# mLSTM heads: low parts of filler weights from an accumulating transfer instead of a VectorE subtraction

## The chip, the cores and the metric

The kernel runs on one core of a Trainium2 chip. The metric is the device time of one execution in microseconds (us); lower is better. TensorE multiplies, VectorE and ScalarE do element-wise work, GpSimd does small work and issues some transfers, SyncE issues most transfers. In the profile they are PE (with PEld for its weight loads), DVE, ACT, POOL and SP.

## What is computed

One decoder layer over 512 tokens of width 1024, float32 throughout:

```python
hN = _rmsnorm(x, norm_g[l])
p = _split_in(hN @ w_in[l])
mq = silu(_causal_dwconv(p["m_q"], conv_q_w[l], conv_q_b[l]))
mk = silu(_causal_dwconv(p["m_k"], conv_k_w[l], conv_k_b[l]))
mh = _mlstm(mq, mk, p["m_v"], p["m_i"] + b_igate[l], p["m_f"] + b_fgate[l])   # 4 heads x 256
ya = sigmoid(p["m_o"]) * _head_layernorm(mh, mh_norm_g[l]) * silu(p["m_z"])
...
yb = _nsa(...) * silu(p["n_z"])                                               # 8 heads x 64
merged = sigmoid(p["g_a"]) * (ya @ w_branch_a[l]) + sigmoid(p["g_b"]) * (yb @ w_branch_b[l])
x = x + merged @ w_out[l]
return _rmsnorm(x, final_norm_g)
```

The part that matters here is the mLSTM branch: for each of four heads the projections to queries and keys, a causal convolution of width 4 with SiLU, scores weighted by the gates' decay, and the products with the values.

## The kernel before

**Products in three passes.** TensorE multiplies in a rounded 32-bit format. To keep the precision of float32, each operand is split into a high part, rounded to that format, and a low part, the difference. A product is three: high x high, high x low, low x high. `split(src, hi, lo)` makes the parts: ScalarE copies `src` into `hi` (which rounds it), then VectorE subtracts, `lo = src - hi`.

**Weights.** `weights(src)` loads a 512 KB tile of weights with SyncE into a raw tile (`wr`, three buffers), and calls `split` for the high part (`wh`, four buffers) and the low part (`wl`, four buffers). A raw buffer is free for the next load when both parts are made; a pair `wh`, `wl` is free when TensorE is done with it. In SyncE's queue a load waits for the release of its raw buffer.

**Filler.** The kernel is arranged so that TensorE always has work. Projections that are not urgent stand in a list of jobs, `stream`. A job is a weight tile and 24 products of 512 columns (12 for branch B); `stream.step(n)` emits n products of it between products of the main work, and at the end of a job its `post` step. When a job is started, the weights of the two jobs behind it are fetched (`Stream(2)`).

**The mLSTM stage.** The list of jobs is: for each head h four `conv` jobs (queries and keys, each in two halves e), 16 in all, then eight `branch` jobs for branch B, which share four weight tiles. `conv`'s `post` reads the finished bank, applies bias and convolution (`u`: one ScalarE instruction and three on VectorE), tanh (`th`, ScalarE), the product with it (VectorE), and splits the result into `qkh` (ScalarE) and `qkl` (VectorE). Then, head after head: scores of keys and queries into `ps`, multiplied by the decay `Dm` and split (`Sh`, `Sl`), six filler products after each block; products with the values (`vh`, `vl`) into `pt` and `po`, with norm statistics on VectorE and, on GpSimd, a power that gives the factor `rho` (line 1364); ScalarE or VectorE scales `num` with it; then `values(h + 1)` loads and splits the next head's values through a raw buffer of the same three, filler runs until the next head's keys are ready and `NEXT_FILL` products more, and the head's result is transposed (`yah`, `yal`). Two jobs run before the first head's decay is made, and two after it.

**Order.** In this stage no engine is held to the order of the program, apart from a few instructions (`keep`). A planner orders each engine's instructions by their place in the program and by its own estimate of when their inputs are there; a high part can so be made well before its place in the program, as soon as a pair of buffers is free.

Behind the stage come eight branch-A jobs and the output projection. There the kernel has two accumulating transfers of 512 KB already (`added`), and five of 256 KB (`xo<-late`), issued by GpSimd.

Of the kernel before, what the change touches and what calls it, by code (L numbers as in the profile page):

```python
# [14 lines left out]
AF = mybir.ActivationFunctionType  # L15
OP = mybir.AluOpType
# [47 lines left out]
def build(  # L64
# [23 lines left out]
    pe, pool = Engine(nc.tensor, "pe"), nc.gpsimd  # L88
    act, dve = Engine(nc.scalar, "act"), Engine(nc.vector, "dve")
    A = act.activation  # L90
# [14 lines left out]
    def f(ap):  # L105
        return ap.bitcast(F32)
# [15 lines left out]
    def split(src, hi, lo, eng="a"):  # L122
        if eng == "a":
            A(hi, src, AF.Copy)
        elif eng == "p":
            pool.tensor_scalar(hi, src, 1.0, 1.0, OP.mult, OP.mult)
        else:
            dve.tensor_copy(hi, src)
        dve.tensor_tensor(lo, src, f(hi), OP.subtract)

    wv = w_in[0].rearrange("(k p) c -> p k c", p=128)

    def weights(src, eng="a"):
        nk, n = src.shape[1], src.shape[2]
        raw = wp.tile([128, nk, n], F32, name="wr", tag="wr", bufs=3)
        nc.sync.dma_start(raw, src)
        hi = wp.tile([128, nk, n], F32R, name="wh", tag="wh", bufs=4)
        lo = wp.tile([128, nk, n], F32R, name="wl", tag="wl", bufs=4)
        split(raw, hi, lo, eng)
        return hi, lo  # L140

    def wcols(c0):
        return weights(wv[:, :, c0 : c0 + 128])

    def wwide(view, c0):
        ws = [weights(view[:, k : k + 4, c0 : c0 + 256]) for k in (0, 4)]
        return (lambda k: ws[k // 4][0][:, k % 4, :]), (lambda k: ws[k // 4][1][:, k % 4, :])
# [134 lines left out]
    with tc.tile_pool(name="ph0", bufs=2, side="right") as p0, tc.tile_pool(  # L282
# [4 lines left out]
        raw = sp.tile([128, ND, SW], F32, name="sraw")  # L287
# [967 lines left out]
    def values(h):  # L1255
        v = wp.tile([128, NT, 256], F32, name="wr", tag="wr", bufs=3)
        nc.sync.dma_start(v, vD[:, :, h * 256 : h * 256 + 256])
        vh = mp.tile([128, NT * 258 + 120], F32R, name="vh", tag="vh")[:, : NT * 258]
        vh = vh.rearrange("p (b d) -> p b d", b=NT)
        vl = mp.tile([128, NT, 256], F32R, name="vl", tag="vl")  # L1260
        vv[h] = vh, vl
        pool.memset(f(vh[:, :, 256:257]), 1.0)
        pool.memset(f(vh[:, :, 257:258]), 0.0)
        split(v, vh[:, :, 0:256], vl)
# [7 lines left out]
    def branch(base, j, yh, yl, nk):  # L1272
        def gen(w):
            o = 0 if nk == ND else (j % 2) * 128
            ps = PP()
            yield from passes(
                ps, lambda k: w[0][:, k, o : o + 128], lambda k: w[1][:, k, o : o + 128],
                lambda k: yh[:, k], lambda k: yl[:, k], nk,
            )
            s = halves.pop((base, j))  # L1280
            if base == GB:
                if not merged:
                    merged.append(pers.tile([128, ND, T], F32, name="mB", tag="hTh"))
                dve.scalar_tensor_tensor(merged[0][:, j], s, 1.0, ps, OP.add, OP.mult)
            else:
                keep(dve.scalar_tensor_tensor(s, s, 1.0, ps, OP.add, OP.mult))
                merge(j, s)

        def load():
            halves[base, j] = sgp.tile([128, T], F32, name="s", tag="s")  # L1290
            nc.sync.dma_start(halves[base, j], gD[base, j])
            if nk == ND:
                return weights(wav[:, :, j * 128 : j * 128 + 128])
            if j % 2 == 0:
                halves["w"] = weights(wbv[:, :, j * 128 : j * 128 + 256])
            return halves["w"]

        stream.add(load, gen)
# [3 lines left out]
    def decay(h):  # L1302
        pgb = PS()
        sl = sel[:, h : h + 1].broadcast_to([128, 128])
        pe.matmul(pgb, sl, ghl, start=True, stop=True)
        dg = mp.tile([128, T], F32, name="dg", tag="dg")
        dve.tensor_tensor(
            dg.rearrange("p (b t) -> p b t", b=NT), pgb.rearrange("p (b t) -> p b t", b=NT),
            later_only, OP.add,
        )  # L1310
        Dm = mp.tile([128, 1280], F32, name="Dm", tag="Dm")
        for sb in range(NT):
            o, n = KOFF[sb], 512 - sb * 128
            bias = cs[:, sb, h : h + 1]
            A(Dm[:, o : o + 128], dg[:, sb * 128 : sb * 128 + 128], AF.Exp, bias=bias, scale=-1.0)
            if n > 128:
                A(Dm[:, o + 128 : o + n], pgb[:, (sb + 1) * 128 :], AF.Exp, bias=bias, scale=-1.0)
        decayed[h] = Dm
# [6 lines left out]
        branch(GB, j, ybh, ybl, 4)  # L1325
    stream.run(2)
    decay(0)
    stream.run(2)
    values(0)

# [79 lines left out]
            stream.step(6)  # L1410

    stream.drain()
    mlp.__exit__(None, None, None)
    yb_pool.__exit__(None, None, None)

# [255 lines left out]
```

## Time and profile before

| | us |
|---|---|
| median of three runs (605.92 to 607.37) | 606.8 |
| the profiled execution | 607.47 |
| its span, first to last instruction | 605.4 |
| TensorE busy in the span | 591.8 |
| VectorE | 485.8 |
| ScalarE | 350.5 |
| GpSimd | 81.9 |
| mean granted TensorE clock | 0.994 |

A row of an engine names what is written and what is read (`wl<-wr,wh`: a low part made of a raw tile and a high part), with the shape. Nearly all rows bear line 80, which is the wrapper that records the order of instructions, so rows are told apart by their tiles. A busy time is the union of an engine's instructions in the stretch; matmuls are pipelined, so their pace is read from the distance of their starts.

### The profile page before, as it was taken

What the parts mean: (1) busy time and instruction counts of PE and PEld (TensorE: products, weight loads), DVE (VectorE), ACT (ScalarE), POOL (GpSimd) and SP (SyncE); (2) the same over time, 40 slices, a digit from 0 to 9 for tenths busy, and PEclk for the clock granted to TensorE, in tenths of its full rate; (3) what the DMA queues carried; (4) which work ended last, traced back from release to release, by engine and by line L of the source; (5) the groups of instructions that cost most, each with busy time, mean ns of one, the idle gap of its engine ahead of it and who ended that gap; (6) DMA issues with size and microseconds to landing.
All of it is one profiled execution on the core that took longest, in us unless ns stands there. A gap on an engine that the chain in (4) does not pass through costs nothing.

```text
span 605.4 us, 8474 instructions
## 1 busy us (share of the span) xinstructions
PE 591.8 (98%) x2956; PEld 496.6 (82%) x2956; DVE 485.8 (80%) x901; ACT 350.5 (58%) x645; POOL 81.9 (14%) x136
## 2 busy tenths in 40 slices
PE   7999999999999899999999999999999999999995
PEld 6988888888887788888888888888887878888885
DVE  5879889597686688887876866889989897589975
ACT  5855546654457366657666665657665653434564
POOL 3100000000005011414324230001010101010121
PEclk9999999999999899999999999999999999999998
DMA  7956654402046644313132214423133153890633
GB/s 222 337 173 178 204 169 128 150 2 87 18 114 177 152 121 125 106 40 106 39 88 68 72 53 123 139 71 88 53 98 110 39 171 110 281 265 24 209 53 139
DMA packets 86740, 74.17 MB, mean 123 GB/s; under 512 B 5229, under 2 KB 69353, under 8 KB 86698
## 3 DMA queue, kind: packets, MB, share of 16 engines
q1 hardware_dynamic: 85400, 70.94, 39.3%
q0 software_dynamic: 1008, 2.36, 2.1%
q8 instruction: 23, 0.38, 0.3%
q10 hardware_dynamic: 290, 0.33, 0.2%
q14 instruction: 19, 0.16, 0.1%
HBM read 61.36 MB, written 8.45 MB: 115 GB/s over the span
## 4 chain that ended last, share of the span: by engine, by line
PE 57%; DVE 6%; ACT 2%; issue 2%; POOL 1%; POOLq 0%; DVEq 0%; ACTq 0%
PE pp L80 39%; PE ps L80 9%; PE pt L80 5%; PE po L80 4%; DVE u L80 2%; DVE wl L80 1%; DVE xo L80 1%; ACT Dm L80 1%; ACT qkh L80 0%; POOL Xr L824 0%; POOL rho L1364 0%; ACT num L80 0%; DVE yal L80 0%; ACT wh L80 0%; DVE num L80 0%
## 5 line engine op out<-in xcount | busy, mean ns | idle before, releaser
L80 PE MATMUL pp<-hTl,wh 128*128 128x512 f32 x352 | 142.7, 405 | 0.0
L80 PE MATMUL pp<-hTh,wh 128*128 128x512 f32 x352 | 139.3, 396 | 0.0
L80 PE MATMUL pp<-hTh,wl 128*128 128x512 f32 x352 | 139.0, 395 | 0.0
L80 DVE TENSOR_TENSOR wl<-wr,wh 128x1024 fp32r<-128x1024 f32 x56 | 69.2, 1239 | 12.0 <-ACT wh L80 11.8
L80 ACT ACTIVATE wh<-wr 128x1024 fp32r<-128x1024 f32 x56 | 58.5, 1059 | 33.3 <-PE pp L80 23.0
L80 PEld LDWEIGHTS pp<-hTh,wh 128*128 128x128 f32 x352 | 66.4, 189 | 12.8
L80 PEld LDWEIGHTS pp<-hTl,wh 128*128 128x128 f32 x352 | 66.6, 189 | 10.6
L80 PEld LDWEIGHTS pp<-hTh,wl 128*128 128x128 f32 x352 | 66.6, 189 | 10.6
L80 ACT ACTIVATE P<-P,st 128x128 f32<-128x128 f32 (+3 forms) x64 | 35.7, 558 | 28.5 <-DVE st L80 28.3
L1110 POOL TENSOR_SCALAR P<-P,st 128x128 f32<-128x128 f32 (+3 forms) x56 | 38.0, 696 | 91.7 <-DVE st L80 59.0
L80 DVE TENSOR_TENSOR wl<-T,wh 128x1024 fp32r<-128x1024 f32 x28 | 34.0, 1222 | 11.3 <-ACT wh L80 11.2
L80 DVE TENSOR_TENSOR wl<-R,wh 128x1024 fp32r<-128x1024 f32 x28 | 33.9, 1222 | 10.2 <-ACT wh L80 10.2
L80 DVE TENSOR_TENSOR ptl<-pt,pth 128x512 fp32r<-128x512 f32 (+1 forms) x64 | 30.9, 485 | 12.2 <-ACT pth L80 11.6
L80 ACT ACTIVATE wh<-T 128x1024 fp32r<-128x1024 f32 x28 | 29.4, 1056 | 18.3 <-PE pp L80 11.0
L80 ACT ACTIVATE pth<-pt 128x512 fp32r<-128x512 f32 (+1 forms) x64 | 27.5, 429 | 20.3 <-PE pt L80 20.0
L80 DVE SCALAR_TENSOR_TENSOR u<-pp,prm,u 128x511 f32<-128x511 f32 (+2 forms) x48 | 35.7, 743 | 2.6 <-ACT u L80 2.3
L80 ACT ACTIVATE wh<-R 128x1024 fp32r<-128x1024 f32 x28 | 29.1, 1056 | 12.4 <-PE pp L80 5.3
L80 DVE CUSTOM_DVE_ANT_0 P<-ps,cst 128x128 f32<-128x128 f32 (+3 forms) x64 | 30.6, 484 | 5.5 <-PE ps L80 5.3
L80 PE MATMUL ps<-k,Th 128*128 128x256 f32 (+2 forms) x112 | 28.6, 336 | 0.0
L80 PE MATMUL pt<-cst,P 128*128 128x128 f32 x160 | 27.9, 272 | 0.0
L80 PEld LDWEIGHTS pt<-cst,P 128*128 128x128 f32 x160 | 20.8, 140 | 7.1 <-DVE ptl L80 0.3
L80 PE MATMUL pp<-yah,wh 128*128 128x512 f32 x64 | 25.0, 390 | 0.0
(355 smaller groups left out, 1360.8 us busy)
## 6 DMA issues: line engine op xcount, KB each, us to landing
wr<-w_in SPq DMA_DIRECT2D x44, 512.0 KB
R<-w_in SPq DMA_DIRECT2D x24, 512.0 KB
gD<-sg SPq DMA_DIRECT2D x16, 256.0 KB
s<-gD SPq DMA_DIRECT2D x16, 256.0 KB
wr<-w_branch_a SPq DMA_DIRECT2D x8, 512.0 KB
R<-w_out SPq DMA_DIRECT2D x8, 512.0 KB
vD<-cq SPq DMA_DIRECT2D x8, 256.0 KB
wr<-vD SPq DMA_DIRECT2D x4, 512.0 KB
```

The source lines that it names most:

```text
L80: ins = fn(*args, **kw)
L1110: pool.tensor_scalar(pj, pj, st[:, 2, j : j + 1], 1.0, OP.mult, OP.mult)
```

## The change

A switch, `by_dma`, is turned on after the first two conv jobs and the first head's decay, and off when the stage's list of jobs is empty. While it is on, `weights` makes the parts in another way. ScalarE copies the raw tile into the high part as before. Then ScalarE makes a second copy of the raw tile, with the factor -1, into the low part; it is rounded as the first, so that it is the negated high part. Then GpSimd issues a transfer of the raw tile that adds to what stands in the low part: raw - high. VectorE has no part in it.

```diff
+    by_dma = []
+
     def weights(src, eng="a"):
         nk, n = src.shape[1], src.shape[2]
         raw = wp.tile([128, nk, n], F32, name="wr", tag="wr", bufs=3)
         nc.sync.dma_start(raw, src)
         hi = wp.tile([128, nk, n], F32R, name="wh", tag="wh", bufs=4)
         lo = wp.tile([128, nk, n], F32R, name="wl", tag="wl", bufs=4)
-        split(raw, hi, lo, eng)
+        if by_dma:
+            A(hi, raw, AF.Copy)
+            A(lo, raw, AF.Copy, scale=-1.0)
+            pool.dma_start(f(lo), raw, accum_op=OP.add)
+        else:
+            split(raw, hi, lo, eng)
         return hi, lo
...
     stream.run(2)
     decay(0)
+    by_dma.append(True)
     stream.run(2)
     values(0)
...
     stream.drain()
+    by_dma.clear()
     mlp.__exit__(None, None, None)
```

The switch does not reach the values (`values` calls `split` itself), the branch-A weights or the output weights.

## The prediction

> **What bounds the kernel now.** I read the page first, then the times of the engines in the stretch that the change touches, then the waits and the chain there. TensorE is busy 98% of the span.
>
> ```profile
> span 605.4 us, 8474 instructions
> PE 591.8 (98%) x2956; PEld 496.6 (82%) x2956; DVE 485.8 (80%) x901; ACT 350.5 (58%) x645; POOL 81.9 (14%) x136
> ```
>
> The profiled execution took 607.47 us: its span and 2.07 us around it. The median of the runs is 606.8, 0.67 below it. I make the sum as a difference and put it on the median.
>
> The stretch runs from the first high part made after the switch (376) to the first branch-A job (517). The rows are microseconds, then busy time and count for PE, PEld, DVE, ACT and POOL, the granted clock, the DMA share and GB/s.
>
> ```profile
> core 0: us, PE busy (x) PEld busy (x) DVE busy (x) ACT busy (x) POOL busy (x), PEclk, DMA share, GB/s
> 376.00:517.00 141.00, 139.90 (x711) 117.53 (x710) 122.61 (x229) 81.96 (x146) 10.98 (x16) 1.00 0.34 100
> 452.00:464.00 12.00, 11.47 (x56) 9.24 (x54) 11.37 (x15) 8.87 (x13) 0.00 (x0) 1.00 0.43 132
> ```
>
> VectorE is busy 122.61 of 141 us, and 11.37 of the 12 us ahead of the head boundary at 464. But TensorE misses only 141.00 - 139.90 = 1.10 us in the whole stretch. The next rows show where; behind each stands the idle time and what ended it.
>
> ```profile
> 395.90 0.39 PE L80 MATMUL pp<-hTh,wl 128*128 128x512 f32 x1
> 396.34 0.50 PE L80 MATMUL ps<-qkh,qkh 128*128 128x512 f32 x1
> ...
> 462.84 0.39 PE L80 MATMUL pp<-hTh,wl 128*128 128x512 f32 x1
> 463.07 0.40 PE L80 MATMUL pp<-hTh,wh 128*128 128x512 f32 x1
> 464.08 0.50 PE L80 MATMUL ps<-qkh,qkh 128*128 128x512 f32 x1 [0.62 <-ACT qkh L80]
> ...
> 494.62 0.40 PE L80 MATMUL pp<-yb,wh 128*128 128x512 f32 x1
> 495.44 0.50 PE L80 MATMUL ps<-qkh,qkh 128*128 128x512 f32 x1 [0.43 <-ACT qkh L80]
> ```
>
> A 512-column product starts 0.23 us after the one before (462.84 to 463.07), so TensorE is at its pace between the gaps, and a busy TensorE here is a full one. All that the change can win is the gap at the boundaries, where the next head's scores wait for the rounded keys (qkh). By starts the three gaps are 0.44, 1.01 and 0.82 us where the pace is 0.23: 0.21 + 0.78 + 0.59 = 1.58 us. By the idle column it is 0.62 + 0.43 = 1.05. The chain of waits ahead of 464 and 495 says that subtractions are on it:
>
> ```profile
> 454.00 0.18 DVE wl L80
> ...
> 455.88 1.13 DVE wl L80
> ...
> 461.63 1.13 DVE wl L80
> 462.76 0.61 DVE u L80
> ...
> 463.40 0.64 ACT qkh L80
> ...
> 464.08 1.57 PE ps L80 x6
> ...
> 485.44 0.18 DVE wl L80
> ...
> 487.31 1.13 DVE wl L80
> ```
>
> **The change part by part.** Sixteen filler weights are made under the switch. Conv jobs 0 to 3 are fetched before it, so conv 4 to 15 (12 tiles) and the four branch-B tiles go the new way. The rows agree: 20 high parts from 376 on are these 16 and four of branch A, and of the 19 subtractions the last three are branch A's.
>
> ```profile
> L80 DVE TENSOR_TENSOR wl<-wr,wh 128x1024 fp32r<-128x1024 f32 x19 | 23.2, 1221 | 6.1 <-ACT wh L80 6.0
> L80 ACT ACTIVATE wh<-wr 128x1024 fp32r<-128x1024 f32 x20 | 20.9, 1058 | 12.9 <-PE pp L80 12.8
> L1364 POOL TENSOR_TENSOR rho<-va,prm 128x3 f32<-128x3 f32 (+1 forms) x8 | 10.6, 1329 | 92.0 <-DVE va L80 92.0
> ```
>
> VectorE loses 16 x 1.221 = 19.5 us: 122.6 becomes 103. ScalarE gains 16 copies of the same form, 16 x 1.058 = 16.9 us: 82 becomes 99 of 141. Neither sum is time of the kernel; each counts only where TensorE waits behind it.
>
> At 464, three subtractions (the chain has parts of them at 454.00, 455.88 and 461.63) lie in VectorE's queue between the last conv jobs' results and the keys: 3.66 us go, against a gap of 0.62. ScalarE gets three copies there, 3.17 us, and has 12.00 - 8.87 = 3.13 us idle. At 495 two go (485.44 and 487.31, 2.44 us) against 0.43. So the ends for TensorE's idle time at the boundaries are: both gaps close, -1.05; or a copy takes the place of each subtraction on the chain (1.06 for 1.22), about 0. No row decides between them, since the order on ScalarE and VectorE in this stretch is the planner's, made anew. I take the middle, -0.5.
>
> The transfer. The kernel has two of the same size and kind (512 KB, accumulating, on-chip to on-chip) and five of half the size:
>
> ```profile
> R<-R POOLq DMA_DIRECT2D x2, 512.0 KB, 6.4
> ...
> q0 software_dynamic: 1008, 2.36, 2.1%
> ...
> L1474 POOL DMA_DIRECT2D R<-R x2: 865/977/1089, 536.3 to 537.8; - x2
> ...
> DMA to landing us min/median/max: 5.9/6.4/6.9
> ```
>
> GpSimd is busy 0.977 us per issue: 16 x 0.977 = 15.6 us on an engine that is busy 10.98 of 141. What can be hurt is rho (8 in the stretch), on whose result the next transposes hang; behind an issue it waits up to 0.98 us. GpSimd sits idle 92.0 us ahead of these pows and waits for VectorE there, so I count 0; the other end is one issue in front of the first pow of each head, 4 x 0.98 = 3.9. The software queue took 2.1% of 605.4 = 12.7 us of all 16 engines for 2.36 MB; 16 x 0.524 = 8.4 MB cost 45 us, which takes the DMA share of the stretch from 0.34 to about 0.66. There is room, and the transfers will be as slow as the two above, which ran beside loads. I take 6.4 us each.
>
> The low part comes later: copy 1.06 and transfer 6.4 instead of a subtraction of 1.22, about 6.2 us. What covers that is how early weights are made:
>
> ```profile
> 376.13 1.06 ACT L80 ACTIVATE wh<-wr 128x1024 fp32r<-128x1024 f32 x1 [1.13 <-PE pp L80]
> 377.10 0.76 ACT L80 ACTIVATE u<-pp,prm 128x512 f32<-128x512 f32 x1
> 377.76 1.05 ACT L80 ACTIVATE vh<-wr 128x1024 fp32r<-128x1024 f32 x1
> ...
> 387.26 1.06 ACT L80 ACTIVATE wh<-wr 128x1024 fp32r<-128x1024 f32 x1 [0.67 <-PE pp L80]
> 388.23 0.61 ACT L80 ACTIVATE th<-u 128x512 f32<-128x512 f32 x1
> ...
> 390.21 0.63 ACT L80 ACTIVATE qkh<-u 128x512 fp32r<-128x512 f32 x1 [0.70 <-DVE u L80]
> 392.70 1.06 ACT L80 ACTIVATE wh<-wr 128x1024 fp32r<-128x1024 f32 x1 [1.85 <-PE pp L80]
> ...
> 394.19 0.76 ACT L80 ACTIVATE u<-pp,prm 128x512 f32<-128x512 f32 x1
> ```
>
> The high part at 376.13 is conv 4's: it waits until conv 0's products free one of the four pairs of buffers. TensorE reaches conv 4 when conv 3 is done, when ScalarE reads its bank (u at 394.19). With u and vh ahead of the new copy the low part lands at 376.13 + 1.06 + 0.76 + 1.05 + 1.06 + 6.4 = 386.5: 7.7 us early. This is the densest stretch, since later jobs share TensorE with scores and values, and the lead is longer. So the late low part costs 0; past 7.7 us more, each microsecond would be one of TensorE.
>
> The Trainium skill, "DMA: Bandwidth & Descriptors", section on the anatomy of one DMA on the SWDGE path, fits such a transfer as 2.0 us and the bytes at 436 GB/s, which would be 3.2 us here (an estimate from that page). The trace has 5.9 and 6.9 for the accumulating ones, twice that, and the trace decides; by the page the low part lands 3.2 us sooner, the sum stays -0.5, and the first rival below is gone.
>
> The raw buffer (three of them) is held longer. The next load on SyncE's queue waits for its release:
>
> ```profile
> 378.48 2.16 SPq L136 DMA_DIRECT2D wr<-w_in  x2
> 389.61 0.37 SPq L136 DMA_DIRECT2D wr<-w_in  x1
> 390.61:391.61 1.00, 1.00 (x7) 0.81 (x6) 0.96 (x3) 0.23 (x1) 0.00 (x0) 1.00 0.71 173
> 391.61:392.61 1.00, 1.00 (x6) 0.84 (x5) 0.96 (x2) 0.00 (x0) 0.00 (x0) 1.00 1.09 329
> 392.61:393.61 1.00, 1.00 (x6) 0.83 (x5) 0.40 (x1) 0.91 (x1) 0.00 (x0) 1.00 0.08 23
> ```
>
> A load moves its data 1 to 3.4 us after its issue (389.61, over by about 393). Conv 6's load, the first of the two at 378.48, waits for conv 4's transfer: 386.5 instead, there at 389.9, and its high part (387.26) is 2.6 us late. ScalarE idles 0.70 + 1.85 = 2.55 us before the next high part at 392.70, so this is made good there; conv 6 itself is multiplied after conv 4 and 5. I count 0, with 2.6 as the other end. Behind these loads on SyncE's queue stand the loads of v and of the stored gates; both are issued a head or two jobs ahead of their use, so I count 0, and if one is late it is a wait like that of rival (4).
>
> The sum: -0.5 at the boundaries, 0 for the rest: 607.47 - 0.5 = 607.0 for a profiled execution, 606.8 - 0.5 = 606.3 for the median, -0.08%. A measurement of this kernel tells about 0.2% (1.2 us) from no change.
>
> **The rivals.** (1) Slower: ScalarE stands still for a raw tile. Place: conv 6's high part at 387.26, ahead of th, u and qkh in ScalarE's order. It decides if the raw tile is there more than 2.55 us late, or if the copies also fill that idle time: then qkh at 395.65, for which TensorE already waits at 396.34, moves by the whole delay, 2.6 us, so 606.8 + 2.6 = 609.4. For it: the load's release moves from a 1.22 us subtraction to a 6.4 us transfer. Against it: the planner can put th and u first.
> (2) Faster by over 0.2%: all three gaps close, -1.58: 605.2. For it: VectorE is the fullest engine ahead of both late boundaries. Against it: ScalarE's idle time there is just as long as its new copies.
> (3) Nothing moves: the copy takes the subtraction's place on the chain: 606.8.
> (4) Low parts or rho late: transfers crowd with the loads, or a pow stands behind an issue that waits for ScalarE. One low part 2 us past its lead, or two pows each 0.98 us later, give about 608.8. Against it: the 7.7 us of lead and GpSimd's empty queue.
>
> **How the numbers follow.** The forecast (-0.2 to -1.05) has 0.36, (3) 0.17, (2) 0.20, (1) 0.17, (4) 0.10. The first two are within 0.2%: 0.53; faster 0.20, slower 0.27. The range goes from (2), a little under 605.2, to (1): 605.0 to 609.4; what lies beyond is less than 2 in 10. The likeliest alone: 605.7 to 606.8.
>
> **What would show it.** In the stretch: VectorE near 103 us and ScalarE near 99; sixteen transfers from GpSimd landing in 5 to 8 us; TensorE's idle time under 1.1 us, and no product that waits for a transfer (right) or rows where qkh comes later and TensorE's gap grows (rival 1), where a product waits for the transfer of wl or a num for rho (rival 4). I am wrong if the planner, with its new estimates, orders TensorE's filler so that more than a microsecond opens anywhere, or if the time moves outside this stretch.

## The result and the profile after

The changed kernel is slower: 611.88 us (median of five runs, 611.31 to 612.29) against 607.04 for the kernel before on the same chip. The ratio is 1.0084, with a 95% interval of 1.007 to 1.0097. The prediction was 606.3, with a range of 605.0 to 609.4, so both its sign and its range were wrong. The profiled execution took 611.87 us.

The head of the page after, then the row of the stretch (microseconds, then busy time and count for PE, PEld, DVE, ACT and POOL, the granted clock, the DMA share, GB/s):

```profile
span 610.1 us, 8510 instructions
PE 593.7 (97%) x2956; PEld 498.2 (82%) x2956; DVE 470.9 (77%) x885; ACT 365.7 (60%) x661; POOL 94.2 (15%) x152
```

```profile
376.00:517.00 141.00, 136.52 (x680) 115.01 (x679) 105.36 (x211) 94.18 (x159) 21.88 (x30) 0.98 0.65 151
```

VectorE fell from 122.6 to 105.4 us here, ScalarE rose from 82.0 to 94.2, and the DMA share from 0.34 to 0.65. TensorE's idle time, however, rose from 1.10 to 4.48 us. The rows of TensorE after (start, length, engine, and in brackets the idle time ahead of a row with what ended it) show where:

```profile
405.99 0.55 PE L80 MATMUL pt<-vh,Sh 128*128 128x258 f32 x1 [4.28 <-ACT Sh L80]
...
498.69 0.50 PE L80 MATMUL ps<-qkh,qkh 128*128 128x512 f32 x1 [0.20 <-ACT qkh L80]
```

Both boundary gaps are all but closed (0.62 and 0.43 before; only 0.20 left, at the second). In their place there is one new stall of 4.28 us, in the first head, ahead of its products with the values. The chain of waits across it:

```profile
389.55 5.44 DMA wl<-wr
394.99 0.02 SPq L138
395.01 0.04 issue
395.05 7.52 DMA wr<-w_in
...
402.65 1.06 ACT wh L80
403.71 0.67 ACT u L80
404.38 0.94 ACT wl L80
405.32 0.53 ACT Sh L80
405.85 0.14 issue
405.99 1.22 PE pt L80 x3
```

The reader is to see four links. Conv 6's transfer, issued at 389.55, holds its raw buffer until 394.99. Only then can SyncE issue conv 8's load, at 395.05 where the kernel before issued it at 389.61, and that load takes 7.52 us. ScalarE stands at conv 8's high part until 402.65, and behind it in ScalarE's fixed order are u, wl and `Sh`. `Sh` is the split score that TensorE waits for. The waits of SyncE's queue from 376 to 410 and ScalarE's row at the end of the wait say the same:

```profile
SPq L138 <- DMA wl<-wr: 21.6, 4, 9.0
```

```profile
402.65 1.06 ACT L80 ACTIVATE wh<-wr 128x1024 fp32r<-128x1024 f32 x1 [4.60 <-DMA wr<-w_in]
```

Why that load took 7.52 us is in the queues' shares while conv 7's transfer moves its data (398.5 to 400.5: packets, MB, share of the 16 engines):

```profile
DMA packets 201, 0.43 MB, mean 216 GB/s; under 512 B 0, under 2 KB 109, under 8 KB 201
## 3 DMA queue, kind: packets, MB, share of 16 engines
q0 software_dynamic: 92, 0.38, 94.0%
q1 hardware_dynamic: 109, 0.06, 13.0%
```

The software queue (q0) carries the transfer, the hardware queue (q1) the load. The two moved nearly the same number of packets, 92 and 109; in w_after (below), where the same pair meets, it is 94 and 96 from 400.0 to 402.0. But the transfer's packets carry some 4 KB each and the load's some 0.5 KB (0.38 MB / 92 and 0.06 MB / 109), so the transfer had 94% of the engines' time and the load 0.06 MB in 2 us. The Trainium skill, "DMA: Bandwidth & Descriptors", section on queues, rings and completion order, states that an engine takes turns between its queues packet by packet. The near-equal counts agree with turns of the profile's packets. The page's packet holds some 9 to 17 descriptors, and the runs do not show whether the two are the same.

One more loss follows the stall. The granted clock is the third figure from the right:

```profile
406.00:412.00 6.00, 6.00 (x18) 5.08 (x19) 5.14 (x14) 2.66 (x7) 0.48 (x1) 0.50 0.48 90
412.00:418.00 6.00, 6.00 (x37) 5.33 (x37) 4.20 (x15) 2.41 (x6) 1.08 (x3) 0.99 0.32 87
```

TensorE is "busy" in all of the first 6 us, but with 18 products where the next 6 us hold 37. The clock is at half there.

### The profile page after: what moved, and what is told of

It is laid out like the page before. It is cut to its first block, busy times and chain, and to the rows that moved or that the text cites. A ratio compares the mean times of both kernels' runs of the same rounds, so it can differ in the third digit from the quotient of the medians.

```text
span 610.1 us, 8510 instructions
## 1 busy us (share of the span) xinstructions
PE 593.7 (97%) x2956; PEld 498.2 (82%) x2956; DVE 470.9 (77%) x885; ACT 365.7 (60%) x661; POOL 94.2 (15%) x152
## 4 chain that ended last, share of the span: by engine, by line
PE 58%; DVE 3%; ACT 2%; DMA 2%; issue 1%; POOL 1%; POOLq 0%; DVEq 0%; ACTq 0%; SPq 0%
PE pp L80 40%; PE ps L80 8%; PE pt L80 6%; PE po L80 4%; DMA wr<-w_in 1%; DMA wl<-wr 1%; DVE u L80 1%; DVE xo L80 1%; DVE wl L80 1%; ACT wh L80 1%; POOL Xr L831 0%; ACT Dm L80 0%; ACT wl L80 0%; POOL fr L1544 0%; ACT u L80 0%
## 5 line engine op out<-in xcount | busy, mean ns | idle before, releaser
L80 DVE TENSOR_TENSOR wl<-wr,wh 128x1024 fp32r<-128x1024 f32 x40 | 49.7, 1247 | 6.1 <-ACT wh L80 6.0
L144 POOL DMA_DIRECT2D wl<-wr x16 | 14.2, 888 | 75.2 <-ACT wl L80 44.8
```

The costliest lines, as they stand in the source:

```text
L80: ins = fn(*args, **kw)
L144: pool.dma_start(f(lo), raw, accum_op=OP.add)
```

## The experiments

The theory after the result was a conjunction of three things: conv 8's load is late because conv 6's transfer holds the raw buffer; the load is slow because conv 7's transfer runs beside it; and ScalarE's order puts the high part that waits for it ahead of `Sh`. Rivals were that ScalarE's added copies or the planner's new order cost the time without any transfer, and that the buffers alone do it.

### No transfers, everything else kept (nodma)

```diff
             A(lo, raw, AF.Copy, scale=-1.0)
-            pool.dma_start(f(lo), raw, accum_op=OP.add)
```

The low part is then the negated high part; the addition is left out.

> The changed kernel without the sixteen transfers: the second copy is made, and the low part stays the negated high part (the adding is left out). Theory (the held raw buffer and the slow load): no wait for the load, 605.5 to 606.8. Rival A (the extra copies on ScalarE): stays at 611 to 612. Rival O (the order that the planner makes with the copies in it costs the time): 609 to 612.

606.19 us, ratio 0.9983 (0.9965 to 1.0). The row of the stretch:

```profile
376.00:517.00 141.00, 140.66 (x714) 118.37 (x713) 108.84 (x215) 97.44 (x164) 8.65 (x14) 1.00 0.34 101
```

ScalarE has all its copies (97.4 us), and TensorE misses 0.34 us of 141. Here, and in raws3 below, ScalarE's order around conv 8's high part is that of the changed kernel (wh, u, wl, `Sh`). So the copies and the new order alone cost nothing; these rivals fall, and the loss needs the transfers.

### Three raw buffers of their own (raws3)

```diff
-        raw = wp.tile([128, nk, n], F32, name="wr", tag="wr", bufs=3)
+        own = by_dma and by_dma[0].tile([128, nk, n], F32, name="wr", tag="wr", bufs=3)
+        raw = own if by_dma else wp.tile([128, nk, n], F32, name="wr", tag="wr", bufs=3)
...
-    by_dma.append(True)
+    by_dma.append(mp)
```

> The changed kernel, with three raw buffers of their own for the sixteen tiles under the switch (so that a load does not wait for an earlier tile's transfer). Theory (the raw tile of conv 8 comes late because its buffer is held by conv 6's transfer, and ScalarE stands still for it): ScalarE's wait of 4.60 us for the load and TensorE's idle 4.28 us near 406 go, the half clock after it too; 606.0 to 606.8. Rival A (ScalarE's sixteen extra copies): unchanged, 611.9. Rival C (the transfers crowd the loads, whatever the buffers): still over 610.

606.88 us, ratio 0.9988 (0.9975 to 1.0). The transfers still take 4.6 to 8.3 us, but the stall at 406 is gone:

```profile
376.00:517.00 141.00, 140.01 (x710) 117.70 (x709) 107.04 (x213) 96.09 (x163) 22.88 (x30) 1.00 0.67 159
```

```profile
379.67 1.06 ACT L80 ACTIVATE wh<-wr 128x1024 fp32r<-128x1024 f32 x1 [2.31 <-DMA wr<-w_in]
```

TensorE's idle time is back at 0.99 us, and its longest gap is 0.48. ScalarE waits for a load twice, 2.31 us here and 1.05 us at 431.35, and no stall of TensorE follows from it. So the held buffer is necessary for the loss.

### The same buffers without the change (b_raws3), and with it from conv 8 on (from_c8_raws)

Before, with the three raw buffers of `mp` for the same tiles; and the change from conv 8 on (as in from_c8, below) with them.

> The kernel before (all parts split on ScalarE and VectorE) with three raw buffers of their own for the sixteen tiles: a control for the run with the same buffers under the switch. Theory: raw buffers bind nothing before the change, 606.4 to 607.4, the same as before. If more buffers are a gain by themselves, 605 or less, and the earlier run would have hidden a loss of the transfers under it.

> The best version so far (switch from conv 8 on) with the three raw buffers of its own as well. Theory: the load that ScalarE still waited for (0.99 us at 429 with the switch from conv 8 on) is early now; nothing else is left to win, 604.6 to 605.8, the same as without the buffers. If held buffers still cost in the later stretch, 604.5 or less.

607.17 us, ratio 1.001 (0.9996 to 1.0024), and 607.16, ratio 1.0005 (0.9989 to 1.0022). More raw buffers alone give the kernel before nothing: its two gaps stay (0.60 and 0.43 us), and one of 0.39 opens ahead of the first head's scores. So they hid no loss of the transfers in raws3. With the change from conv 8 on, a gap of 0.35 us opens at the same place. That run missed its expectation (604.6 to 605.8), and the gap is too small for the difference; the rest stays open. Raw buffers cure the stall; where there is none, they gain nothing.

### Transfers in small pieces (pad)

```diff
-        lo = wp.tile([128, nk, n], F32R, name="wl", tag="wl", bufs=4)
+        lo = wp.tile([128, nk, n + 1 if nk == 8 else n], F32R, name="wl", tag="wl", bufs=4)[:, :, :n]
```

A low part with a spare column makes the transfer's pieces 512 bytes, as small as the load's. It does so for the twelve conv tiles; branch B's four stay as they were.

> The changed kernel with the rows of the low part's tile for the conv weights one element longer (129 for 128), so that the transfers of these twelve tiles go in pieces of 512 bytes, as the loads do, instead of 4 KB. Theory of shares (a load in pieces of 512 bytes beside a transfer in pieces of 4 KB gets about one byte in nine): the load of conv 8 lands in some 5 us instead of 7.5, and TensorE's idle time near 406 shrinks to 2 us or less; 608 to 610, unless the small pieces make the transfers much longer (over 9 us), and then 612 or more. If pieces do not matter: 611.9 and 4.3 us of idle time as before.

626.13 us, ratio 1.0306 (1.0289 to 1.0324): much worse. The transfers' median landing rises from 5.3 to 6.7 us, and their share of the engines in the stretch from 33.9% (after, 2304 packets) to this:

```profile
q0 software_dynamic: 13056, 8.39, 47.2%
...
wl<-wr POOLq DMA_DIRECT2D x16, 512.0 KB, 6.7
```

```profile
407.77 1.06 ACT L80 ACTIVATE wh<-wr 128x1024 fp32r<-128x1024 f32 x1 [4.84 <-DMA wr<-w_in]
```

```profile
411.10 0.55 PE L80 MATMUL pt<-vh,Sh 128*128 128x258 f32 x1 [4.49 <-ACT Sh L80]
```

A stall of the same length stands at the same place, and others join it (1.42, 1.46, 1.60 and 1.35 us between 472 and 512). But it is made in another way, as the chain of waits shows:

```profile
396.84 6.92 DMA wl<-wr
...
403.82 3.86 DMA wr<-w_in
```

Conv 8's load takes 3.86 us instead of 7.52. It had moved most of its data before conv 7's transfer, issued at 404.08, moved any (from 406.5 to 407.0 the load's queue has 297 packets and the transfer's 29, its first). So the load was not crowded, and the run says nothing of even turns. What makes the stall is the release alone: conv 6's transfer, issued at 396.84, holds the buffer until 403.76, when ScalarE has stood free since 402.93 (407.77 less 4.84). The expectation was missed: the load came sooner than the 5 us that it named, yet the idle time did not shrink to 2 us, and the time is 626 though no transfer took over 9 us (4.6 to 8.0). The run changes several things at once: pieces, their number, and GpSimd's issue, busy 1.41 us on the mean instead of 0.89. It shows that longer transfers with the same three buffers stall more often, and that a release that is late enough needs no crowded load.

### Conv 7 as before (no_c7) and conv 6 as before (no_c6)

```diff
-        if by_dma:
+        if by_dma and by_dma.append(True) is None and len(by_dma) - 2 not in (3,):
```

`(3,)` leaves out the fourth tile under the switch, conv 7; no_c6 has `(2,)`. The tile left out is split by VectorE as before.

> The changed kernel with conv 7 alone split as before: conv 8's load still waits for conv 6's transfer, but no transfer moves beside it. Theory of the slow load: it lands in 3.4 to 4 us instead of 7.5, ScalarE waits 0.5 to 1.5 us instead of 4.6, TensorE idles under 1 us there: 605.5 to 607. If the late issue alone makes the loss, the wait stays over 3 us and the time at 610 or more.

> The changed kernel with conv 6 alone split as before (15 tiles under the switch; ScalarE still has the high part of conv 8 ahead of Sh in its order). Theory of the held buffer: conv 8's load is issued some 5 us sooner, as soon as conv 6's subtraction is done, and the whole loss goes: 605.0 to 606.8, ScalarE waits under 0.6 us for that load. If the extra copies or the new order cost the time, one tile of sixteen cannot matter: 611 to 612.

no_c7: 606.42 us, ratio 0.9997 (0.998 to 1.0014). Conv 8's load goes out as late as in the changed kernel:

```profile
395.65 1.00 SPq L138 DMA_DIRECT2D wr<-w_in  x2
```

```profile
399.09 0.76 ACT L80 ACTIVATE u<-pp,prm 128x512 f32<-128x512 f32 x1
399.79 1.06 ACT L80 ACTIVATE wh<-wr 128x1024 fp32r<-128x1024 f32 x1
```

ScalarE makes conv 8's high part at 399.79 with no wait, 4.14 us after the load's issue. No transfer runs beside this load (397.5 to 399.5):

```profile
q1 hardware_dynamic: 1281, 0.65, 115.0%
```

The load's queue, with conv 8's and conv 9's loads on it, moves 0.65 MB in 2 us where in the changed kernel it moved 0.06. At this lateness the issue alone loses nothing; the crowded load is necessary too. The planner also put u ahead of the high part here. In the changed kernel's own order a load of 4.14 us would have been there at 399.19, 1.14 us after ScalarE was free (402.65 less 4.60), and some 0.8 us of TensorE's gap would have stayed; this is an estimate from these rows.

no_c6: 607.73 us, ratio 1.0016 (1.0002 to 1.0031), above the 605.0 to 606.8 expected. Conv 8's load goes out 2.9 us sooner, and the stall at 406 is gone:

```profile
392.13 0.37 SPq L138 DMA_DIRECT2D wr<-w_in  x1
```

Conv 7's transfer, issued at 396.19, moves its data after this load's, so that the early issue takes away the crowding too. A smaller gap of rival (1)'s shape opens at the next boundary, where in ScalarE's order a high part and u stand ahead of qkh:

```profile
463.64 0.50 PE L80 MATMUL ps<-qkh,qkh 128*128 128x512 f32 x1 [1.46 <-ACT qkh L80]
```

```profile
461.36 1.05 ACT L80 ACTIVATE wh<-wr 128x1024 fp32r<-128x1024 f32 x1
462.31 0.76 ACT L80 ACTIVATE u<-pp,prm 128x512 f32<-128x512 f32 x1
462.97 0.62 ACT L80 ACTIVATE qkh<-u 128x512 fp32r<-128x512 f32 x1
```

Take away the late release or the crowded load, and the 4.28 us of the changed kernel are gone. The third condition, ScalarE's order, costs nothing by itself (nodma, raws3); the late load with another order was not run, so that part is read from the rows and not tested.

### From conv 8 on (from_c8, from_c8_again)

```diff
-        if by_dma:
+        if by_dma and by_dma.append(True) is None and len(by_dma) - 2 not in (0, 1, 2, 3):
```

Conv 4 to 7 are split as before; twelve tiles go the new way.

> The change for twelve of the sixteen tiles: conv 4 to 7 are split as before, the switch works from conv 8 on. Theory (the loss is the dense stretch before 406 alone, and the rest of the change closes gaps at the two later boundaries): 605.8 to 606.6, TensorE idle under 0.6 us in the stretch. Rival A: three quarters of the loss, about 610.5. Rival O: anywhere from 606 to 611.

> The transfers from conv 8 on only, as in from_c8, beside the three others on one chip. Theory (gaps at the boundaries closed and nothing lost): 605.2 to 606.2, its executions in the two groups of the kernel before, each about 1 us lower. If from_c8's 605.21 was chance, it comes out at 606.8 to 607.2.

605.21 us, ratio 0.996 (0.9942 to 0.9977), below the 605.8 to 606.6 expected, and again 605.83, ratio 0.9975 (0.9965 to 0.9984), as expected. This version is 0.25 to 0.4% faster than the kernel before, and so faster than both. The row of the stretch in the first:

```profile
376.00:517.00 141.00, 140.66 (x715) 118.54 (x714) 112.43 (x220) 94.08 (x160) 20.62 (x26) 1.00 0.60 147
```

0.34 us idle instead of 1.10: on TensorE's rows the boundary gaps are what the change can win, some 0.8 us. The medians differ by more, 1.8 and 1.4 us; how many executions ran at half clock near 199 us enters there. The two profiled executions of this one kernel have spans of 602.8 and 604.4 us. They differ near 199 us, after an idle time of some 2.6 us (2.2 in pad) that all these kernels but the two with twelve spare products have there. The row of the first, then of the second:

```profile
199.00:201.00 2.00, 2.00 (x13) 1.74 (x12) 1.72 (x6) 0.68 (x2) 0.00 (x0) 1.00 0.69 148
```

```profile
199.00:201.00 2.00, 2.00 (x5) 1.55 (x6) 1.65 (x6) 0.48 (x2) 0.00 (x0) 0.50 0.68 134
```

In one the clock stayed whole, in the other it was at half (13 products against 5). So the same idle time costs some 1.6 us in one execution and nothing in the next.

### Spare products in that idle time (w_before, w_from_c8)

```diff
+    spare = PO()
+    for _ in range(12):
+        pe.matmul(spare, hTh[:, 0, :128], hTh[:, 0, :], start=True, stop=True)
     activated(0, u0)
```

> The kernel before with twelve spare products of 128x512 (their result is used by nothing) ahead of the first gate's sigmoid, so that TensorE has work in the 2.6 us in which it stands still near 198.3 us. Theory (the spread of the kernel before, about 605.1 in some executions and about 607.2 in others, comes from whether this idle time makes one window of 3.4 us run at half clock): no row at 0.50 near 199 to 202 us, and a median of 605.0 to 605.5, with none of the runs grouped near 607.2. Rival (the spread comes from elsewhere): the median stays near 607 and both groups are there. If the twelve products themselves delay the work behind them, up to 0.5 us more.

> The transfers from conv 8 on only (conv 4 to 7 split as before), with the same twelve spare products ahead of the first gate's sigmoid. Both theories of the stall say the same here: no stall at 406 us. If the half clock near 199 us and the gaps at the boundaries are two separate losses, they add up: 604 us (605.2 for the spare products less about 1 us for the gaps). If the gain of from_c8 (605.21) came from its executions without the half clock alone, it comes out like the kernel before with the spare products, 605.2.

609.99 us, ratio 1.0044 (1.0028 to 1.006), and 608.52, ratio 1.0026 (1.0011 to 1.0041). The theory's number was missed: the spare products fill the idle time at 198, but the stand-still only moves. In w_before it comes at 205, and the half clock with it:

```profile
205.12 0.41 PE L80 MATMUL ps<-u,w2t 128*128 128x64 f32 x2 [2.62 <-ACT both L80]
```

```profile
206.40:209.60 3.20, 3.20 (x9) 2.52 (x8) 0.72 (x2) 0.00 (x0) 0.00 (x0) 0.50 0.27 55
```

TensorE had done its filler first and stood still for another gate instead. So these runs do not show that the spread goes away with the idle time. What they do give is a like-for-like pair of profiled executions: w_from_c8 has the same gap (2.61 us at 205.12) and half clock (0.51 from 206.4 to 209.6). The median with the transfers from conv 8 on is 1.5 us lower (608.52 against 609.99), but the two intervals overlap, so the pair supports the gain and does not prove it. The rows of the stretch, of w_before and of w_from_c8:

```profile
376.00:520.00 144.00, 142.91 (x724) 120.07 (x723) 124.47 (x232) 82.74 (x148) 11.07 (x16) 1.00 0.35 100
```

```profile
376.00:520.00 144.00, 143.76 (x729) 121.11 (x728) 113.36 (x221) 94.85 (x161) 20.80 (x28) 1.00 0.59 145
```

0.85 us of idle time less, of a difference of 1.1 us in the spans (608.3 and 607.2).

### Spare products in the stall (w_after)

```diff
+        if h == 0:
+            spare = PO()
+            for _ in range(20):
+                pe.matmul(spare, hTh[:, 0, :128], hTh[:, 0, :], start=True, stop=True)
```

> The changed kernel with twenty spare products of 128x512 in the first head (their result is used by nothing): three between the scores and seventeen, some 3.9 us, right ahead of the product of vh and Sh, which is where TensorE stands still for 4.28 us. ScalarE's order around conv 8's high part is that of the changed kernel. Theory (the stall costs its 4.28 us and, through the half clock of 405.3 to 412.1 us, some 3.4 us more): conv 8's high part still waits some 4 us for its load, the clock stays at 0.96, and the time is 608 to 609. Rival (the half clock costs nothing, since ScalarE or VectorE sets the pace in those 6.8 us): 611.5 to 612. Rival (the three products ahead of the scores shift the load away from the transfer): conv 8's load takes 4 us or less, and the run tells nothing of the clock.

612.63 us, ratio 1.0086 (1.007 to 1.0103), against the 608 to 609 of the theory; the rival's 611.5 to 612, in which the half clock costs nothing, was nearer. ScalarE waits for its load as in the changed kernel, 4.55 us, and the clock stays whole:

```profile
403.90 1.06 ACT L80 ACTIVATE wh<-wr 128x1024 fp32r<-128x1024 f32 x1 [4.55 <-DMA wr<-w_in]
```

```profile
407.24 0.36 PE L80 MATMUL pt<-vh,Sh 128*128 128x258 f32 x1 [0.31 <-ACT Sh L80]
...
411.56 0.28 PE L80 MATMUL po<-vh,Sh 128*128 128x258 f32 x1
...
436.17 0.50 PE L80 MATMUL ps<-qkh,qkh 128*128 128x512 f32 x1 [0.99 <-ACT qkh L80]
```

```profile
407.00:412.00 5.00, 4.60 (x25) 3.93 (x26) 3.90 (x8) 1.88 (x6) 0.73 (x1) 1.00 0.55 105
```

From the first product with the values to the first `po`, TensorE takes 4.32 us (407.24 to 411.56, the last row at full clock), with three filler products more in between than the changed kernel has. There the same way took 6.14 us (405.99 to this row):

```profile
412.13 0.30 PE L80 MATMUL po<-vh,Sh 128*128 128x258 f32 x1
```

Three products at 0.23 us are 0.69, so the half clock cost TensorE 6.14 - 4.32 + 0.69 = 2.5 us. But the kernel is not faster: the three spare products that ran ahead of the stall cost 0.7, since as many filler products moved behind it, and 0.99 comes back as a gap at 436, where ScalarE and VectorE are behind. Its profiled execution, unlike that of the changed kernel, also has the half clock near 199, which puts it 1.3 us back before the stretch (conv 6's high part at 387.37 against 386.07). Its span is 611.0 us against 610.1, so from there on it is 0.4 us shorter. The clock's part is shown on TensorE's rows and in no time of a kernel; what it is worth at the end lies somewhere between 0 and 2.5 us and stays open.

## Why the prediction was wrong, point by point

**The spans.** 610.1 - 605.4 = 4.7 us. Conv 6's high part, well ahead of the stall, starts 1.2 us sooner than before (386.07 against 387.26), since this execution of the changed kernel has no half clock near 199. Then: -1.2, +4.28 for the stall, +2.5 for the half clock behind it, and -0.85 for the boundary gaps (1.05 to 0.20) give 4.7. The last two are readings of TensorE's rows, so this is a ledger and not a second proof.

**The boundaries (-0.5).** Right in sign, and at its far end: 0.62 and 0.43 became nothing and 0.20, -0.85 us. The middle was taken for want of a row; the runs lie near the end at which both gaps close.

**Engine sums.** VectorE 103 forecast, 105.4 measured in a window in which the stall put off some of its work, and 108.8 without the stall (nodma); so less was saved in this window than the 19.5 forecast, and no run was made to say why. ScalarE 99, measured 94.2 there and 97.4 without the stall (nodma).

**The transfers (6.4 us each, 45 us of all engines).** They landed in 4.5 to 7.0:

```profile
L144 POOL DMA_DIRECT2D wl<-wr x16: 855/863/1094, 377.8 to 494.2; - x16
...
DMA to landing us min/median/max: 4.5/5.3/7.0
```

33.9% of 141 us is 47.8 us of all engines, and the DMA share came out at 0.65 for 0.66. GpSimd's issues took 0.89 us each for the 0.98 forecast. The sums held; a single transfer was mostly shorter than the 6.4 us taken, and the shortest lies below the 5 to 8 us named as a sign. The 3.2 us estimated from the Trainium skill, "DMA: Bandwidth & Descriptors", section on the anatomy of one DMA, is below all sixteen.

**Low parts (0) and rho (0).** Right: no product in the stretch waits for a transfer of wl or for rho; TensorE's only gaps are the two shown. Rival (4) fell.

**The raw buffer (0, other end 2.6).** This is the step that failed. The mechanism was there, and rival (1) had it: the load waits for a transfer, and ScalarE stands still in its order with TensorE's input behind it. Three things in it were wrong.
- The place. Only conv 6's high part was followed, where there were 2.55 us of idle time to swallow the delay. It was not late at all (386.07): the two loads of that time went out at 380.00 and by 383.3, not at 386.5. The buffers turn over every three tiles, and the delay bit two conv tiles on, at conv 8, where `Sh` was queued behind it.
- The size. "A load moves its data 1 to 3.4 us after its issue" was read from a load with its queue alone on the engines. Beside a transfer it took 7.52 us. The DMA share of 0.66 was taken as "room", but it is a mean: for two microseconds the engines were full and 94% went to the other queue. In the sentence "the transfers will be as slow as the two above, which ran beside loads" the contention was priced for the transfers and not for the loads.
- What comes behind. A stall of 4.28 us on TensorE was followed by half clock, 2.5 us on its rows. The prediction gave no idle time of TensorE a price beyond its own length. The profile before had the pattern: 2.59 us of idle time at 198.34 and 3.4 us at half clock after it.

The Trainium skill, "TensorE: Matmul & The Clock Gate", Part 1, has the clock judged in free-running windows of 3413 ns. The runs agree as far as they go: the stretches at half clock were 3.4 us in w_before and 6.8 in the changed kernel, and the same 2.6 us of idle time led to one in one execution and to none in the next.

Rival (1)'s 609.4 stopped at a delay of 2.6 us; with the measured 4.28 it would have been 606.8 + 4.28 = 611.1, without the clock and the boundaries. The range ended at that price because each delay was bounded with the other parts as they stood in the trace of before. The prediction's sign of being wrong, more than a microsecond opening anywhere, did come, but not through the order of TensorE's filler that it named for it.

## What to carry to other kernels

When a buffer's release moves from an engine's instruction to a transfer, follow every later user of that ring of buffers, not only the next one: find the place where the waiting instruction has the critical engine's input behind it. If the release comes late enough, that alone makes a stall (pad). Price a load by what runs beside it: here a load in 0.5 KB packets got 0.06 MB in 2 us beside a transfer in 4 KB packets, while the mean DMA share of the stretch was 0.65. And switch such a mechanism on only where there is slack: the same change from conv 8 on was faster than both kernels.

## What the runs showed of the hardware that was not expected

- A 512 KB load took 7.52 us beside an accumulating transfer of 512 KB, with 13.0% of the engines' time against 94.0% in the two microseconds in the middle; with no transfer beside it, it was there 4.14 us after its issue at the latest (no_c7).
- With twelve of the sixteen transfers in 512-byte pieces they are slower: median 6.7 us instead of 5.3, 47.2% of the engines' time instead of 33.9% for the same 8.39 MB (the windows are equally long, 141 us), and 1.41 us of GpSimd per issue on the mean instead of 0.89.
- An idle time of TensorE of 2.6 us was followed by 3.4 us at half clock in some executions of a kernel and not in others: 1.6 us between two spans of from_c8, twice the 0.8 us that the change wins on TensorE's rows.
